# Gate columns split inside one stationary tile, new tokens' gates by one broadcast matmul, decay rows by DMA: one change to a hybrid decoder layer on Trainium2

## The chip, the cores and the metric

One NeuronCore of a Trainium2 chip. Its engines run unsynchronised, each through its own queue in order: TensorE (PE in the profile, with PEld for its weight loads), VectorE (DVE), ScalarE (ACT), GpSimd (POOL) and SyncE (SP), which here only starts DMAs. The metric is the device time of one execution in microseconds; lower is better.

## The reference

One layer of a decoder for 512 prompt tokens and 8 new tokens (520 columns), model width 1024: a half-step SwiGLU network, a token mixer, a second half-step SwiGLU network, with RMSNorm before and after each. The mixer projects its input once and runs two branches, four retention heads and four gated-delta heads of 128 channels. The change lies in the gates of the gated-delta heads:

```python
proj = (h @ w_in).astype(f32)
rq, rk, rv, rg, conv_in, gz, ga, gb, gate_r, gate_g = jnp.split(proj, idx, axis=-1)
...
beta = jax.nn.sigmoid(gb)
g_gdn = -jnp.exp(gdn_a_log.astype(f32)) * jax.nn.softplus(ga + gdn_dt_bias.astype(f32))
o_g, s_gdn_new = gated_delta_chunked(gq, gk, gv, g_gdn, beta, s_gdn.astype(f32))
```

`ga` and `gb` are four columns each, one per head. The chunked form needs `G`, the running sum of `g` within a chunk, both down the partitions (`gcol`) and as a row spread over all partitions, for the decay mask exp(G_i - G_j). New tokens need their own exp(g) and beta on all partitions.

## The kernel before, in words

Activations lie transposed: channels on partitions, the 520 tokens along the row, in two halves of 260 columns. Every product with weights is done in three passes of the fast four-byte format: weights and activations are split into a high and a low part, and high x high, high x low and low x high are summed in PSUM (`passes`, lines 404 to 410, so most matmuls have line 408, 409 or 410). A weight unit of 1024 x 128 is loaded by SyncE into one of two raw buffers, then `split` (line 340) makes the high part by a cast on ScalarE (line 350) and the low part by a subtract on VectorE (line 351). Splits are emitted by `prefetch`, up to two units ahead of the product (`AHEAD`).

The order of all work is written out by one Python program. `product` issues a unit's 48 matmuls and calls `tick` after every six. Side work is generators: each `yield n` means "go on n ticks later", and in a tick the generators' instructions are appended to their engines' queues. So a position on a queue is fixed by the tick, and an engine that falls behind meets its instructions late but in the same order. A table `LATER` (line 46) adds ticks to numbered steps of named generators, such as step 51 of the second `gdn_head`; a step is counted each time a generator yields a number above zero.

The mixer's first four units are done together by `first_units` (line 701), half by half, while the norm's factors `r` are still being made (`pre_rms`, `inverse_rms`: squares, seven adds on VectorE, line 537, sums `ss` by matmul, line 471, a power on GpSimd, and a broadcast matmul `rb`, line 477). They are: GAB, the gates' unit, in which 8 of 128 columns are used and the rest are zeros; then the key, query and value projections of gated-delta head 0 (CK, CQ, CV). When `r` is there, all four are evacuated in a row. CK, CQ and CV of heads 1 to 3 follow, then the retention units, the output gates and the branch gates. `conv` (line 1261) evacuates a unit (`cin`, line 1268) and convolves it by three VectorE operations (line 1276).

`gate_rows` (line 1164) evacuates 8 rows. `gates` (line 1170), a generator, transposes them (five transposes through line 1162), adds the bias, makes `g` and `beta` in its second step, and in its last step (from line 1214) issues one matmul with the triangle of ones (line 1215) for `gcol`, eight small matmuls that spread one head's new-token `g` or `beta` over 128 partitions (line 1218), and the copies out of PSUM (lines 1226 to 1232). The profile counts a matmul on plain four-byte data as two records, so these are 2 and 16.

`gdn_head` (line 1368) is one generator per head. Heads start their decays 48 ticks apart (`TURN`). `decays` (line 1235) spreads the head's `g` columns over the partitions while summing them, by four 128 x 128 matmuls into a PSUM bank `gbc` (line 1240), and makes from it exp(G) (`eg`), the mask `DT` (line 1247) and `ekd`. Then `inverse` (line 1484) moves blocks through DRAM by SyncE (`s1`, `L`, lines 1493 and 1499), does 31 steps of two small operations on GpSimd (lines 1513, 1514), stores by eight DMAs (line 1519), and reads back. The state is then carried over four chunks: `ks` (line 1447), `pu` (line 1453), `pS` (line 1457) and `S` (line 1459).

Of the kernel before, what the change touches and what calls it, by code (L numbers as in the profile page):

```python
# [15 lines left out]
P = 128  # L16
D = 1024
# [16 lines left out]
KH = KD // 2  # L34
PAD = CONV_W - 1
TURN = 48
WARM = 9
RAW_BUFS, SPLIT_BUFS, AHEAD = 2, 9, 2
SUM_LAG = 6
# [68 lines left out]
def units():  # L108

    out = []  # L110
    for f in (1, 2):
        for m in range(KF):
            if m < PLAIN[f]:
                out += [(f"gu{f}", 2 * m, 0, 8), (f"gu{f}", 2 * m + 1, 0, 8)]
        out += [("seven", f, m, i) for m, i in stream(PLAIN[f])]
        for d in range(KD):
            rest = [(f"dn{f}", d, 8, 15), (f"dn{f}", d, 15, 22)]
            if d in (0, KD - 1):
                out += rest + [(f"dn{f}", d, 0, 8)]
            else:  # L120
                out += rest
                if d % 2 == 0:
                    out += [("down7", f, d - 1, i) for i in range(7)]
        if f == 1:
            n = len(proj_order()) - 2 * KD
            out += [("win", i, 0, 8) for i in range(n)]
            for i in range(n, n + 2 * KD, 2):
                out += [("win", i, 0, 8), ("win", i + 1, 0, 8), ("wbr", (i - n) // 2, 0, 8)]
            out += [("wo", m, 0, 8) for m in range(KD)]
    return out  # L130

# [39 lines left out]
class Kernel:  # L171
# [95 lines left out]
    def load_to(self, j):  # L267

        nc, a = self.nc, self.a
        while self.raw_next < min(self.group[min(j, len(self.unit_list))] + RAW_BUFS, self.group[-1]):  # L270
            u = self.unit_list[self.first_of[self.raw_next]]
            if u[0] == "seven":
                w, m = a[f"gu{u[1]}"], u[2]
                s1, s3, a22 = self.begun.pop((u[1], m), None) or self.begin_pair(u[1], m)
                t = self.raw.tile([P, KD, P], F32, tag="raw", name=self.name("raw"))
                nc.sync.dma_start(out=t, in_=w[2 * m])
                t = [t[:, 0:KH], s3, None, a22, t[:, KH:KD], s1, None]
            elif u[0] == "down7":
                t = []
                for d in (u[2], u[2] + 1):  # L280
                    raw = self.raw.tile([P, KD, P], F32, tag="raw", name=self.name("raw"))
                    nc.sync.dma_start(out=raw, in_=a[f"dn{u[1]}"][d, :, 0:KD, :])
                    t += [raw[:, 0:KH], raw[:, KH:KD]]
            else:
# [119 lines left out]
    def passes(self, w, k, xhl, ps, first, last, more=False):  # L404
        hi, lo = w
        xh, xl = xhl
        mm = self.nc.tensor.matmul
        mm(ps, hi[:, k, :], xh, start=first, stop=False, skip_group_check=more)  # L408
        mm(ps, hi[:, k, :], xl, start=False, stop=False, skip_group_check=more)  # L409
        mm(ps, lo[:, k, :], xh, start=False, stop=last, skip_group_check=more)  # L410

# [752 lines left out]
    def gate_rows(self, ps):  # L1164
        rows = self.slot("rows", (P, TOK))
        for hf, (c0, n) in enumerate(HALVES):
            self.nc.vector.tensor_tensor(rows[0:8, c0 : c0 + n], ps[hf][0:8], self.r[hf][0:8], ALU.mult)
        return rows

    def gates(self, rows):  # L1170
# [2 lines left out]
        yield 4  # L1173
        pt = self.bank("gt")
        for i in range(NCH):
            self.tr(pt[:, i * 8 : i * 8 + 8], rows[0:8, i * P : (i + 1) * P])
        self.tr(pt[0:DEC, 32:40], rows[0:8, SEQ:TOK])
        ga = c.tile([P, 5, H], F32, name="ga")
        gb = c.tile([P, 5, H], F32, name="gb")
        nc.gpsimd.memset(ga, 0.0)  # L1180
        nc.gpsimd.memset(gb, 0.0)
        dt = self.vec[:, V_DT : V_DT + H]
        ptv = pt[:, 0:40].rearrange("p (c g) -> p c g", g=8)
# [29 lines left out]

        pc = self.bank("gc")
        nc.tensor.matmul(pc[:, 0:16], self.triu, g[:, 0:4, :], start=True, stop=True)
        for i, src in enumerate((g, beta)):
            for h in range(H):
                nc.tensor.matmul(
                    pc[:, 16 + (i * H + h) * DEC : 16 + (i * H + h + 1) * DEC],
                    src[0:DEC, 4, h : h + 1].to_broadcast([DEC, P]),  # L1220
                    self.ident[0:DEC, 0:DEC],
                    start=True,
                    stop=True,
                )
        self.gcol = c.tile([P, NCH, H], F32, name="gcol")
        nc.vector.tensor_copy(self.gcol, pc[:, 0:16])
        self.dgb = c.tile([P, 2, H, DEC], F32, name="dgb")
# [7 lines left out]
    def decays(self, h):  # L1235

        nc = self.nc
        pb = self.bank("gbc")
        for i in range(NCH):
            nc.tensor.matmul(  # L1240
                pb[:, i * P : (i + 1) * P], self.g[:, i, h : h + 1].to_broadcast([P, P]), self.triu, start=True, stop=True
            )
        eg = self.slot("eg", (P, NCH, P))
        nc.scalar.activation(eg, pb, AF.Exp)
        dt = self.slot("DT", (P, NCH, P))
        for i in range(NCH):
            nc.vector.scalar_tensor_tensor(
                out=dt[:, i, :],
                in0=pb[:, i * P : (i + 1) * P],
                scalar=self.gcol[:, i, h : h + 1],  # L1250
                in1=self.negm,
                op0=ALU.subtract,
# [1 line left out]
            )  # L1254
        nc.scalar.activation(dt, dt, AF.Exp)
        e = self.ekd[:, :, h]
        nc.vector.tensor_tensor(e, pb.rearrange("p (c i) -> p c i", i=P)[:, :, P - 1], self.gcol[:, :, h], ALU.subtract)
        nc.scalar.activation(e, e, AF.Exp)
        return eg, dt

# [107 lines left out]
    def gdn_head(self, h, q, k, v):  # L1368
# [408 lines left out]
def layouts(i):  # L1777
# [15 lines left out]
    blocks = []  # L1793
    for kind, h in proj_order():
        if kind == GAB:
            b = np.zeros((D, P), f)
            b[:, 0:8] = w[:, 4096:4104]
        else:
            b = w[:, start[kind] + h * P : start[kind] + (h + 1) * P]
# [78 lines left out]
```

## Time and profile before

| | |
|---|---|
| median of 3 runs | 1218.39 us (1217.87 to 1218.42) |
| span of the profiled execution | 1218.5 us |
| TensorE busy | 1189.1 us, 9937 matmul records |
| VectorE busy | 899.6 us |
| ScalarE, GpSimd busy | 573.7 us, 277.1 us |
| mean granted TensorE clock | 0.990 |
| HBM traffic | 139 GB/s over the span |

A row of a timeline gives start and duration in microseconds, the engine, the line of the kernel, the operation, and output <- input by the program's names; a matmul's shape follows, "x8" counts records, and brackets tell how long the engine stood before it and for whom. Durations of matmuls are modelled and overlap: what counts is the distance from one start to the next. A row of the waits gives who waited for whom, the total, the number and the longest. A row of the chain gives start, duration and what ran. A row of the windows gives, for a stretch, the length, each engine's busy time with its records, the granted clock, the DMA share and GB/s.

### The profile page before, as it was taken

Reading aid. Unit: us, or ns where it says so; the run is one execution under the profiler, and the core shown is the slowest. Engines: PE = TensorE matmul, PEld = TensorE weight load, DVE = VectorE, ACT = ScalarE, POOL = GpSimd, SP = SyncE. Lnnn points to the kernel's source line nnn. Section 1 sums busy time; section 2 is a strip of 40 time slices with the busy share of each in tenths; the row PEclk is TensorE's granted clock in tenths of the full one; section 3 lists DMA queues with packets and bytes.
Section 4 is the critical chain, followed back from the end, with each engine's and each line's share of the span. In section 5 each row is a group of like instructions: output and inputs, shape, how many; then the busy total and the mean of one; then the engine's idle time right before and its main releaser. Section 6 shows DMA issues by size and latency. Waiting matters only on the chain.

```text
span 1218.5 us, 25498 instructions
## 1 busy us (share of the span) xinstructions
PE 1189.1 (98%) x9937; PEld 1176.9 (97%) x9937; DVE 899.6 (74%) x1933; ACT 573.7 (47%) x1195; POOL 277.1 (23%) x502
## 2 busy tenths in 40 slices
PE   8999999999999999999999999999999999999995
PEld 7999999999999999999999999998999999999994
DVE  8988888776548787877666667546888888867554
ACT  6655666553335564313234334334565666653330
POOL 4211111000005148745541112203311111000003
PEclk8999999999999999999999999999999999999998
DMA  6787777133352533332444564342587777332352
GB/s 191 210 203 178 192 176 185 45 100 96 96 171 60 176 105 107 117 97 89 116 133 144 175 195 172 114 157 85 152 229 190 188 183 192 85 92 81 96 168 70
DMA packets 79689, 170.87 MB, mean 140 GB/s; under 512 B 17104, under 2 KB 20016, under 8 KB 79568
## 3 DMA queue, kind: packets, MB, share of 16 engines
q1 hardware_dynamic: 67280, 144.95, 37.4%
q0 software_dynamic: 12288, 24.29, 11.7%
q8 instruction: 78, 1.28, 0.4%
q14 instruction: 43, 0.35, 0.1%
HBM read 157.37 MB, written 11.83 MB: 139 GB/s over the span
## 4 chain that ended last, share of the span: by engine, by line
PE 88%; DVE 6%; ACT 2%; issue 1%; DMA 1%; POOL 1%; SPq 0%; DVEq 0%; ACTq 0%; POOLq 0%
PE sv L408 10%; PE sv L409 10%; PE sv L410 10%; PE p L408 7%; PE p L410 7%; PE p L409 7%; PE dn L408 7%; PE dn L409 7%; PE dn L410 7%; DVE wlo L351 2%; PE br L408 1%; PE br L409 1%; PE br L410 1%; PE g L409 1%; PE g L410 1%
## 5 line engine op out<-in xcount | busy, mean ns | idle before, releaser
L408 PE MATMUL p<-xhl,whi 128*128 128x260 f32 x784 | 231.0, 295 | 0.0
L409 PE MATMUL p<-xhl,whi 128*128 128x260 f32 x784 | 222.0, 283 | 1.4 <-DVE xhl L506 1.4
L410 PE MATMUL p<-xhl,wlo 128*128 128x260 f32 x784 | 221.3, 282 | 1.7 <-DVE wlo L351 1.7
L351 DVE TENSOR_TENSOR wlo<-raw,whi 128x1024 fp32r<-128x1024 f32 (+2 forms) x121 | 142.3, 1182 | 37.7 <-ACT whi L350 35.9
L408 PE MATMUL sv<-th,w 128*128 128x260 f32 x592 | 167.2, 282 | 0.5 <-ACT q L833 0.5
L409 PE MATMUL sv<-tl,w 128*128 128x260 f32 x592 | 167.1, 282 | 0.0
L410 PE MATMUL sv<-th,w 128*128 128x260 f32 x592 | 167.0, 282 | 0.0
L409 PEld LDWEIGHTS p<-xhl,whi 128*128 128x128 f32 x784 | 148.4, 189 | 2.0 <-DVE xhl L506 1.8
L410 PEld LDWEIGHTS p<-xhl,wlo 128*128 128x128 f32 x784 | 147.9, 189 | 2.1 <-DVE wlo L351 2.1
L408 PEld LDWEIGHTS p<-xhl,whi 128*128 128x128 f32 x784 | 148.1, 189 | 0.7
L350 ACT CAST whi<-raw 128x1024 fp32r<-128x1024 f32 (+2 forms) x121 | 116.4, 971 | 31.3 <-DMA raw<-dn_in 16.9
L369 DVE TENSOR_TENSOR w<-s,w 128x512 fp32r<-128x512 f32 x148 | 101.5, 688 | 37.9 <-ACT w L368 36.5
L307 POOL DMA_DIRECT2D s<-gu_in x74 | 65.1, 973 | 282.4 <-DMA s<-gu_in 143.8
L410 PE MATMUL dn<-hh,wlo 128*128 128x260 f32 x448 | 126.6, 283 | 1.2 <-DVE wlo L351 1.2
L408 PE MATMUL dn<-hh,whi 128*128 128x260 f32 x448 | 127.0, 283 | 0.0
L409 PE MATMUL dn<-hl,whi 128*128 128x260 f32 x448 | 126.7, 283 | 0.0
L409 PE MATMUL sv<-xhl,w 128*128 128x260 f32 x444 | 125.5, 283 | 0.0
L408 PE MATMUL sv<-xhl,w 128*128 128x260 f32 x444 | 125.4, 282 | 0.0
L410 PE MATMUL sv<-xhl,w 128*128 128x260 f32 x444 | 125.0, 281 | 0.0
L408 PEld LDWEIGHTS sv<-th,w 128*128 128x128 f32 x592 | 111.4, 188 | 0.9 <-ACT q L833 0.7
L410 PEld LDWEIGHTS sv<-th,w 128*128 128x128 f32 x592 | 111.6, 188 | 0.0
L409 PEld LDWEIGHTS sv<-tl,w 128*128 128x128 f32 x592 | 111.2, 188 | 0.0
(408 smaller groups left out, 3230.4 us busy)
## 6 DMA issues: line engine op xcount, KB each, us to landing
raw<-gu_in SPq DMA_DIRECT2D x50, 512.0 KB, 5.0
raw<-win_in SPq DMA_DIRECT2D x49, 512.0 KB, 3.6
s<-gu_in SPq DMA_DIRECT2D x74, 256.0 KB, 5.7
s<-gu_in POOLq DMA_DIRECT2D x74, 256.0 KB, 5.4
raw<-dn_in SPq DMA_DIRECT2D x32, 448.0 KB, 3.4
a<-gu_in SPq DMA_DIRECT2D x37, 256.0 KB, 5.9
x<-x SPq DMA_DIRECT2D x32, 260.0 KB, 5.1
raw<-dn_in SPq DMA_DIRECT2D x16, 512.0 KB, 3.7
```

Source lines behind the costliest of these rows:

```text
L307: self.nc.gpsimd.dma_start(out=out, in_=term, accum_op=ALU.add)
L350: self.nc.scalar.copy(hi[:, ks], t[:, ks])
L351: self.nc.vector.tensor_tensor(lo[:, ks], t[:, ks], hi[:, ks].bitcast(F32), ALU.subtract)
L369: nc.vector.tensor_tensor(w[:, 1], t[i], w[:, 0].bitcast(F32), ALU.subtract)
L408: mm(ps, hi[:, k, :], xh, start=first, stop=False, skip_group_check=more)
L409: mm(ps, hi[:, k, :], xl, start=False, stop=False, skip_group_check=more)
L410: mm(ps, lo[:, k, :], xh, start=False, stop=last, skip_group_check=more)
```

## The change

Four parts.

1. GAB is no longer a 128-column weight unit with a low part of its own. Its 8 columns are loaded as a small tile; high parts go into columns 0 to 7 and low parts into columns 8 to 15 of one stationary tile, the rest of which is zeroed. `passes` gets `lo` as None and issues two passes. Rows 0 to 7 and 8 to 15 of the result are added after the transposes, in `gates`. The unit list is renumbered; the unit still counts as two split buffers.
2. In the last step of `gates`, the eight small matmuls become one: VectorE multiplies `g` and `beta` of the new tokens with an identity into `diag`, and one matmul with ones spreads all 64 columns.
3. A second product with the triangle gives `G` as 16 rows of 128; VectorE copies them out (`growc`) and SyncE stores them to a DRAM tile `gscr`.
4. `decays` has no matmuls. Each head reads its four rows from `gscr`, repeated over 128 partitions (256 KB), by a SyncE DMA that is issued `ROWS_EARLY` = 12 ticks before the decays. Where there are not twelve ticks, as at head 0, which takes its turn at once, the decays come twelve ticks after the read. `LATER` is not edited.

```diff
@@ passes
+        if lo is None:
+            mm(ps, hi[:, k, :], xl, start=False, stop=last, skip_group_check=more)
+            return
@@ split
+        if self.unit_list[j][0] == "gab":
+            self.load_to(j)
+            t = self.loaded[self.group[j]]
+            both = self.whl.tile([P, KD, P], F32R, tag="w", name=self.name("both"))
+            self.started(j)
+            self.split_done[j] = (both, None)
+            self.nc.scalar.activation(both, self.ones.unsqueeze(1).to_broadcast([P, KD, P]), AF.Copy, scale=0.0)
+            self.nc.scalar.copy(both[:, :, 0:8], t)
+            self.nc.vector.tensor_tensor(both[:, :, 8:16], t, both[:, :, 0:8].bitcast(F32), ALU.subtract)
+            return
@@ gates, after the transposes (now of 16 rows)
-        nc.vector.tensor_tensor(ga[:, 0:4, :], ptv[:, 0:4, 0:4], dt.unsqueeze(1).to_broadcast([P, 4, H]), ALU.add)
-        nc.vector.tensor_tensor(ga[0:DEC, 4, :], ptv[0:DEC, 4, 0:4], dt[0:DEC], ALU.add)
-        nc.vector.tensor_copy(gb[:, 0:4, :], ptv[:, 0:4, 4:8])
-        nc.vector.tensor_copy(gb[0:DEC, 4, :], ptv[0:DEC, 4, 4:8])
+        nc.vector.tensor_copy(sb[:, 0:4, :], ptv[:, 0:4, :])
+        nc.vector.tensor_copy(sb[0:DEC, 4, :], ptv[0:DEC, 4, :])
+        nc.vector.tensor_tensor(ga, sb[:, :, 0:4], sb[:, :, 8:12], ALU.add)
+        nc.vector.tensor_tensor(gb, sb[:, :, 4:8], sb[:, :, 12:16], ALU.add)
+        nc.vector.tensor_tensor(ga, ga, dt.unsqueeze(1).to_broadcast([P, 5, H]), ALU.add)
@@ gates, last step
         nc.tensor.matmul(pc[:, 0:16], self.triu, g[:, 0:4, :], start=True, stop=True)
+        nc.tensor.matmul(pc[0:16, P : 2 * P], g[:, 0:4, :], self.triu, start=True, stop=True)
+        diag = self.small("dg", [P, 2, H, DEC])
+        eye = self.ident[0:DEC, 0:DEC].unsqueeze(1).to_broadcast([DEC, H, DEC])
         for i, src in enumerate((g, beta)):
-            for h in range(H):
-                nc.tensor.matmul(
-                    pc[:, 16 + (i * H + h) * DEC : 16 + (i * H + h + 1) * DEC],
-                    src[0:DEC, 4, h : h + 1].to_broadcast([DEC, P]),
-                    self.ident[0:DEC, 0:DEC],
-                    start=True,
-                    stop=True,
-                )
+            nc.vector.tensor_tensor(diag[0:DEC, i], src[0:DEC, 4, :].unsqueeze(2).to_broadcast([DEC, H, DEC]), eye, ALU.mult)
+        nc.tensor.matmul(pc[:, 16:80], self.ones[0:DEC, :], diag[0:DEC], start=True, stop=True)
+        grow = self.slot("growc", (16, P))
+        nc.vector.tensor_copy(grow, pc[0:16, P : 2 * P])
+        self.gscr = self.dram.tile([NCH, H, P], F32, name="gscr")
+        nc.sync.dma_start(out=self.gscr.rearrange("c h i -> (c h) i"), in_=grow)
@@ decays: its four matmuls become a read
+    def decay_rows(self, h):
+
+        t = self.slot("gbc", (P, NCH, P))
+        self.nc.sync.dma_start(out=t, in_=self.gscr[:, h, :].unsqueeze(0).to_broadcast([P, NCH, P]))
+        return t
@@ gdn_head
-        if turn > self.now:
-            yield turn - self.now
-        eg, DT = self.decays(h)
+        if turn - ROWS_EARLY > self.now:
+            yield turn - ROWS_EARLY - self.now
+        rows = self.decay_rows(h)
+        yield max(turn, self.now + ROWS_EARLY) - self.now
+        eg, DT = self.decays(h, rows)
```

More of the change, by code (lines that the diff above doesn't have):

```diff
@@ L36 @@
 TURN = 48
+ROWS_EARLY = 12
 WARM = 9
@@ L125, in units @@
             n = len(proj_order()) - 2 * KD
-            out += [("win", i, 0, 8) for i in range(n)]
+            out += [("gab", 0, 0, 8)] + [("win", i, 0, 8) for i in range(n - 1)]
             for i in range(n, n + 2 * KD, 2):
-                out += [("win", i, 0, 8), ("win", i + 1, 0, 8), ("wbr", (i - n) // 2, 0, 8)]
+                out += [("win", i - 1, 0, 8), ("win", i, 0, 8), ("wbr", (i - n) // 2, 0, 8)]
             out += [("wo", m, 0, 8) for m in range(KD)]
@@ L283, in load_to @@
                     t += [raw[:, 0:KH], raw[:, KH:KD]]
+            elif u[0] == "gab":
+                t = self.slot("gabw", (P, KD, 8))
+                nc.sync.dma_start(out=t, in_=a["gab"])
             else:
@@ L1166, in gate_rows @@
         for hf, (c0, n) in enumerate(HALVES):
-            self.nc.vector.tensor_tensor(rows[0:8, c0 : c0 + n], ps[hf][0:8], self.r[hf][0:8], ALU.mult)
+            self.nc.vector.tensor_tensor(rows[0:16, c0 : c0 + n], ps[hf][0:16], self.r[hf][0:16], ALU.mult)
         return rows
@@ L1233, in gates, with decays @@
         self.ekd = c.tile([P, NCH, H], F32, name="ekd")
-    def decays(self, h):
-        nc = self.nc
[L1238 to L1242, printed above, removed]
+    def decay_rows(self, h):
+        t = self.slot("gbc", (P, NCH, P))
+        self.nc.sync.dma_start(out=t, in_=self.gscr[:, h, :].unsqueeze(0).to_broadcast([P, NCH, P]))
+        return t
+    def decays(self, h, pb):
+        nc = self.nc
         eg = self.slot("eg", (P, NCH, P))
@@ L1248, in decays @@
                 out=dt[:, i, :],
-                in0=pb[:, i * P : (i + 1) * P],
+                in0=pb[:, i, :],
                 scalar=self.gcol[:, i, h : h + 1],
@@ L1256, in decays @@
         e = self.ekd[:, :, h]
-        nc.vector.tensor_tensor(e, pb.rearrange("p (c i) -> p c i", i=P)[:, :, P - 1], self.gcol[:, :, h], ALU.subtract)
+        nc.vector.tensor_tensor(e, pb[:, :, P - 1], self.gcol[:, :, h], ALU.subtract)
         nc.scalar.activation(e, e, AF.Exp)
@@ L1795, in layouts @@
         if kind == GAB:
[L1796 to L1799, printed above, removed]
+            out["gab"] = asc(w[:, 4096:4104].reshape(KD, P, 8).transpose(1, 0, 2))
+            continue
+        b = w[:, start[kind] + h * P : start[kind] + (h + 1) * P]
         blocks.append(b.reshape(KD, P, P).transpose(1, 0, 2))
```

10 lines of the change are left out of this document (5 added, 5 removed).

## The prediction

> **What bounds the kernel now.** I read the page first, then what TensorE waits for.
>
> ```profile
> span 1218.5 us, 25498 instructions
> PE 1189.1 (98%) x9937; PEld 1176.9 (97%) x9937; DVE 899.6 (74%) x1933; ACT 573.7 (47%) x1195; POOL 277.1 (23%) x502
> PE p L410 <- DVE wlo L351: 1.7, 2, 1.4
> ```
>
> TensorE is busy for 98% of the span, so matmuls taken out should shorten it, unless TensorE comes to wait for another engine where they stood. Its waits are few today; the 1.4 us one for `wlo` lies in the stage that the change edits. So I read the chain of waits there, then VectorE and TensorE in order of time.
>
> ```profile
> 399.21 0.66 DVE rows L1167 x2
> ...
> 411.18 1.23 DVE wlo L351
> 412.45 0.39 PE p L410
> ...
> 420.71 1.88 PE gc L1218 x16
> ```
>
> From 399 to 412 us VectorE carries the chain: the four leading units get their factors `r` all at once, and it works off their evacuations and convolutions. TensorE runs ahead and is caught once, at 412.45. How far behind VectorE stays is seen where the gates' last stage stands (first fence TensorE, second VectorE):
>
> ```profile
> 420.42 0.29 PE L1215 MATMUL gc<-gg,cst 128*128 128x16 f32 x2
> ...
> 422.51 2.08 PE L1240 MATMUL gbc<-cst,gg 128*128 128x128 f32 x8
> 424.25 0.57 PE L408 MATMUL p<-xhl,whi 128*128 128x260 f32 x1
> 424.61 0.42 PE L409 MATMUL p<-xhl,whi 128*128 128x260 f32 x1
> 424.82 0.42 PE L410 MATMUL p<-xhl,wlo 128*128 128x260 f32 x1
> ```
>
> ```profile
> 425.57 0.42 DVE L1268 TENSOR_TENSOR cin<-p,rb 128x260 f32<-128x260 f32 x1
> 427.11 2.75 DVE L1276 SCALAR_TENSOR_TENSOR cv<-cin,vec,cv 128x512 f32<-128x512 f32 x3 [0.72 <-ACT cv L1274]
> 429.77 1.23 DVE L351 TENSOR_TENSOR wlo<-raw,whi 128x1024 fp32r<-128x1024 f32 x1
> 430.93 0.16 DVE L1226 COPY gcol<-gc 128x16 f32<-128x16 f32 x1
> 431.35 0.19 DVE L1229 COPY dgb<-gc 128x32 f32<-128x32 f32 x1 [0.26 <-ACT dgb L1228]
> ```
>
> TensorE issues the gates' matmuls at 420.42. The first thing that VectorE is given in the same step, the `gcol` copy, runs at 430.93 with no wait before it: VectorE is 10 us behind, on an evacuation, a convolution and a weight split that were emitted earlier. Today that costs nothing, because no matmul of this step reads anything VectorE makes in it. It is this that the change alters.
>
> **Part by part.** *GAB unit.* Its third pass goes: 8 k x 2 halves = 16 matmuls.
>
> ```profile
> 379.00 0.39 PE L410 MATMUL p<-xhl,wlo 128*128 128x260 f32 x1 [0.33 <-DVE wlo L351]
> 391.56 1.51 DVE L537 TENSOR_TENSOR sq<-sq,sq 128x520 f32<-128x520 f32 x2
> 393.45 0.28 PE L410 MATMUL p<-xhl,wlo 128*128 128x260 f32 x1
> 393.57 1.02 PE L471 MATMUL ss<-ones,sq 128*87 128x1 f32 x12
> ```
>
> Matmuls of this form start 0.12 us apart (393.45 to 393.57), so on paper 1.92 us go. The first half's 0.96 us are worth nothing: they lie ahead of 379.00, where TensorE stands for another unit's split whenever it arrives. The second half's 0.96 us bring the sums `ss` to 392.61, but the last `sq` add ends at 393.07; with hand-over I take 393.12. From `ss` the chain runs through `r` to 412.45 without TensorE's products, so 0.45 us is what everything after gains. The new split (a zero fill and a narrow copy on ScalarE, a narrow subtract on VectorE) replaces a full cast and subtract long before the unit is due; the load shrinks; neither was waited for by TensorE. I cost them at zero; were that cover gone, about one such subtract, 1.23, would be exposed.
>
> *Gate rows, transposes, gates.* The transposes stay five; wider ones cost nothing, by L1215, whose 16 columns take 0.11 a record where L1218's 8 take 0.12. VectorE gets five small operations for four ahead of the last stage: +0.15 us, by the 0.16 of `gcol`. ScalarE, 47% busy, may load its exponential table twice more, since head 0's exponentials move away from this step's; no matmul waits for that.
>
> *The last stage.* Out go the 16 records of L1218 and head 0's 8 of L1240 (422.51). In come a second product of `g` with `triu` (2 records, 0.22 by L1215) and one broadcast matmul of `diag`. The two multiplies that make `diag` are emitted in the same step, so they stand on VectorE's queue exactly where `gcol` stands now, behind the 429.77 split. TensorE arrives at 420.42 - 0.45 + 4 records x 0.11 = 420.41. VectorE arrives at 430.93 - 0.45 + 0.15 = 430.63 and needs about 0.3 for two operations like `dgb`'s 0.19: 430.9. TensorE stands for 10.5 us. Behind the waiting matmul is the rest of this unit's product, that is, all of TensorE's work; who would wait for that, VectorE and ScalarE, are draining their own backlog, so nothing on them gets faster for it. With 0.3 for the matmul the product resumes at 431.2, where it resumed at 424.25: +6.95.
>
> *Clock.* The windows view (granted clock third from the right):
>
> ```profile
> 15.00:19.70 4.70, 4.70 (x23) 4.70 (x23) 4.70 (x11) 3.82 (x11) 1.64 (x3) 0.50 0.43 122
> 19.80:24.00 4.20, 4.20 (x37) 4.20 (x37) 3.78 (x8) 2.08 (x5) 0.00 (x0) 1.00 0.42 120
> 422.60:425.90 3.30, 3.30 (x15) 3.30 (x16) 3.24 (x6) 2.93 (x18) 1.64 (x2) 0.50 0.76 286
> 426.00:440.00 14.00, 14.00 (x121) 14.00 (x121) 11.36 (x32) 10.40 (x29) 5.96 (x8) 1.00 0.27 76
> 13.77 0.59 PE L409 MATMUL g<-xhl,whi 128*128 128x260 f32 x1 [0.62 <-DVE xhl L506]
> ```
>
> After the stretch of tiny matmuls the granted clock fell to 0.50 for 3.3 us; the products from 424.25 to 425.9 ran 0.21 apart (424.61 to 424.82) instead of 0.12: eight of them, 0.75 us lost. That loss goes. But a stand of 10 us must bring the clock down too. What recovery costs is bounded by the two stretches here: 3.3 us at half speed, 1.65 lost; or, from the last start-up wait (13.77) to 19.7, 5.9 us, 3.0 lost. I take the middle, 2.3. Net +1.55. The Trainium skill (TensorE: Matmul & The Clock Gate, Part 1) says the gate opens after one busy window of about 3.4 us; by that alone the loss would be some 1.7, an estimate, and the sum 0.6 lower; the start-up rows show a longer stretch, so the middle stands.
>
> *Heads 1 to 3.* Their broadcasts on TensorE go.
>
> ```profile
> 463.05 1.05 PE L1240 MATMUL gbc<-cst,gg 128*128 128x128 f32 x8
> 463.86 0.37 PE L408 MATMUL p<-xhl,whi 128*128 128x260 f32 x1
> 464.06 0.28 PE L409 MATMUL p<-xhl,whi 128*128 128x260 f32 x1
> 569.11 1.06 PE L1240 MATMUL gbc<-cst,gg 128*128 128x128 f32 x8
> ```
>
> Each takes 0.81 (463.05 to 463.86) and a re-entry 0.08 over pitch (0.20 for 0.12): 0.89, and no wait stands nearby to swallow it. Three: -2.7. The Trainium skill (same page, Back-to-back issue gap) gives about 81 ns per matmul of 128 columns in a stream; by that, an estimate, the 24 records are worth 1.9 and the sum is 0.8 higher. The rows show 0.81 per eight, so they decide.
>
> In their place each head reads 256 KB of rows by SyncE twelve ticks ahead; the nearest rows are the inverse's own broadcast loads:
>
> ```profile
> L1499 SPq DMA_DIRECT2D L<-s x8: 520/551/601, 446.5 to 583.7; - x8
> DMA to landing us min/median/max: 3.1/3.5/4.3
> SPq L1519 <- POOL TT L1524: 11.2, 4, 6.2
> ```
>
> 4.3 us at most against twelve ticks. Turns are 48 ticks apart and head 0's stood at 422.51, head 1's at 463.05, so a tick is 0.85 and twelve are 10 us: hidden, if SyncE is free. For head 0 the write of `growc` and the read follow VectorE's 431; any load emitted later is emitted by a product that stood still as well. Zero; its ends are none and the 4 us of the second rival.
>
> *Moved steps.* Head 0 starts twelve ticks later, and each head has one more counted step, so the hand-set corrections of LATER fall one step early. For head 1 the 7 - 3 shortened wait moves to the wait between writing `S` and the matmul that reads it, which falls from 5 ticks to 1.
>
> ```profile
> 599.40 0.39 PE L1467 MATMUL go<-AT,qk 128*128 128x128 f32 x2
> 600.57 0.33 DVE L1459 SCALAR_TENSOR_TENSOR S<-S,egl,pS 128x128 f32<-128x128 f32 x1
> 606.03 0.38 PE L1447 MATMUL ks<-S,cv 128*128 128x128 f32 x2
> ```
>
> One tick of six products (0.72) after 599.62 is 600.35; `S` is done at 600.90: a wait of 0.5. The other corrections move inside loops with slack. Between nothing and 2; I take 0.5.
>
> *Sum.* +6.95 +1.55 -2.7 +0.5 = +6.3 on the profiled 1218.5, which is 0.1 above the median of the three runs. So 1224.7.
>
> **Rivals.** *The matmul finds `diag` ready.* If VectorE reached the last stage with TensorE, the step would cost 0.25 after 420.41, resuming at 420.66 against 424.25 (-3.6), with the 0.75 of clock gone and -2.7 from the heads and 0.5 back: 1211.9. For it speaks that TensorE is 98% busy and loses some 50 records; against it the 430.93 row. It decides by VectorE's lag: gain and loss cross at a wait of about 4.3 us, taking 2.3 for the clock; the rows have 10.5. If the two multiplies slipped in ahead of 425.57, the wait would be near 5, and the time 1219, no change.
>
> *Rows late.* SyncE issues in order. Head 0's inverse, twelve ticks later, puts its eight stores in front of head 2's rows, and such stores waited for GpSimd up to 6.2 us. With that and the 3.5 of landing, head 2's rows would come about 4 us after their turn; ScalarE's exponentials and VectorE stop, and TensorE loses up to those 4 us at the next split it needs: 1228.7. For it speaks the 6.2, against it that splits are made two units ahead, which is why I cost it at zero.
>
> **How the numbers follow.** My forecast 0.74; `diag` ready 0.09; half the wait, no change, 0.07; rows late 0.10. A measurement of this kernel can tell about 0.2% (2.4 us) from no change. Faster 0.09, same 0.08, slower 0.83. The forecast's own range: low with 1.65 for the clock, no extra step and VectorE 1 us sooner, 1222.5; high with 3.0 and 2 us of moved steps, 1226.9. Taking in the late rows, and on the low side a shorter lag: 1221.5 to 1229.5.
>
> **What would show it.** Right: TensorE waits some 10 us for the `diag` tile in one piece near 420 us, the clock at 0.50 for 3 to 6 us after it, the `ss` sums only 0.5 us sooner, `gcol` again near 431, head turns without matmuls. Wrong: no wait at that matmul, or TensorE's stand made up by fewer waits before 600 us, or new waits for the row transfers.

## The result and the profile after

| | before | after |
|---|---|---|
| median, on the same chip | 1218.41 us (1217.87 to 1219.99) | 1235.14 us (1234.54 to 1235.8) |
| ratio, 95% interval | | 1.0139 (1.0126 to 1.0151) |
| profiled execution, span | 1218.5 us | 1234.0 us (time 1235.8) |
| mean granted TensorE clock | 0.990 | 0.985 |

The change makes the kernel slower by 16.7 us. The forecast was slower by 6.3, 1221.5 to 1229.5 at its ends: the sign is right, the size far off. The clock means leave out the first 6.1 us of the kernel before and the first 16.7 us of the kernel after, for which the traces hold no clock record (the windows view prints 1.00); matmuls stand 0.21 us apart there, as they do at half clock. One execution of a kernel in experiment 8, of 2964.56 us, is left out of its ratio.

The page's head for the kernel after (busy time, share of the span, instructions):

```profile
span 1234.0 us, 25386 instructions
PE 1190.7 (96%) x9877; PEld 1177.2 (95%) x9877; DVE 903.6 (73%) x1937; ACT 577.0 (47%) x1198; POOL 275.0 (22%) x501
```

TensorE issues 60 records fewer and its busy time still doesn't fall (1189.1 before). Records that run at half clock last longer (0.42 us instead of 0.28 for a product's matmul in the rows below), so busy time hides a clock loss. The view of waits for TensorE, kernel after:

```profile
PE gc L1239 <- DVE dg L1238: 10.5, 1, 10.5
PE cb L1636 <- POOL gdm L1633: 3.7, 1, 3.7
PE g L426 <- DVE xhl L523: 2.8, 5, 1.0
```

The first line is the stand that was forecast. The second is new and was not: the matmul `cb` of the new tokens' norm waits 3.7 us for a power, `gdm`, on GpSimd. The rest are much as before. TensorE's order of time around both, kernel after:

```profile
418.75 0.37 PE L1233 MATMUL gc<-gg,cst 128*128 128x16 f32 x2
419.06 0.39 PE L1234 MATMUL gc<-cst,gg 128*16 128x128 f32 x2
429.90 0.69 PE L1239 MATMUL gc<-dg,ones 8*128 8x64 f32 x2 [10.45 <-DVE dg L1238]
430.52 0.59 PE L422 MATMUL p<-xhl,whi 128*128 128x260 f32 x1
...
505.93 0.28 PE L427 MATMUL p<-xhl,wlo 128*128 128x260 f32 x1
509.92 0.69 PE L1636 MATMUL cb<-cst,gdm 64*128 64x64 f32 x2 [3.71 <-POOL gdm L1633]
510.53 0.58 PE L422 MATMUL p<-xhl,whi 128*128 128x260 f32 x1
510.91 0.42 PE L426 MATMUL p<-xhl,whi 128*128 128x260 f32 x1
511.13 0.42 PE L427 MATMUL p<-xhl,wlo 128*128 128x260 f32 x1
```

And VectorE at the first of them, kernel after:

```profile
428.41 1.24 DVE L365 TENSOR_TENSOR wlo<-raw,whi 128x1024 fp32r<-128x1024 f32 x1
429.57 0.17 DVE L1238 TENSOR_TENSOR dg<-gg,cst 8x32 f32<-8x32 f32 x1
429.67 0.17 DVE L1238 TENSOR_TENSOR dg<-beta,cst 8x32 f32<-8x32 f32 x1
430.62 0.28 DVE L1241 COPY growc<-gc 16x128 f32<-16x128 f32 x1 [0.78 <-PE gc L1239]
430.83 0.15 DVE L1245 COPY gcol<-gc 128x16 f32<-128x16 f32 x1
```

The two multiplies run directly behind the weight split, where `gcol` stood before. The windows view of after (length, then busy time and records of PE, PEld, DVE, ACT, POOL, then granted clock, DMA share, GB/s) shows, between start-up and the end, three stretches at half clock where before had one of 3.4 us:

```profile
422.90:436.50 13.60, 6.60 (x29) 6.48 (x30) 7.32 (x22) 6.47 (x15) 5.56 (x6) 0.50 0.35 112
436.60:508.20 71.60, 69.61 (x584) 69.25 (x583) 57.98 (x142) 35.72 (x89) 39.49 (x96) 1.00 0.34 98
508.30:515.10 6.80, 5.18 (x23) 5.07 (x24) 2.06 (x10) 0.00 (x0) 5.77 (x19) 0.50 0.35 65
515.20:614.00 98.80, 98.31 (x888) 96.43 (x886) 70.32 (x214) 28.14 (x55) 47.55 (x126) 1.00 0.33 104
614.10:617.40 3.30, 3.30 (x17) 3.23 (x17) 2.28 (x6) 0.88 (x3) 0.00 (x0) 0.50 0.55 144
```

To see where the time comes, I subtract the start of a product's matmul before from the start of the same matmul after (both streams hold the same product matmuls, `p` in the mixer and `sv` in the networks, counted from the last one):

| TensorE's place (time in before) | after minus before, us | step |
|---|---|---|
| first network (52.5 to 236.5) | -1.2 | start-up, put down to the clock (last section) |
| ahead of the gates' last stage (405.2) | -1.65 | GAB -0.45 |
| 25 us past it (449.5) | +8.4 | the stand for `diag` and its clock, +10.05 |
| past head 1's turn (476.9) | +7.6 | its decay matmuls gone, -0.8 |
| ahead of `cb` (496.3) | +7.7 | |
| ahead of head 3's turn (564.9) | +12.25 | +4.55: head 2 -0.8, eight records of the heads' state (`pu`, `pS`, `go`) that come later in this stream -0.9, so `cb`'s stand and its clock +6.25 |
| past it (587.9) | +11.4 | -0.8 |
| past the third stretch at half clock (606.5) | +14.0 | +2.6, of which 1.7 clock and 0.9 those eight records |
| end of the projections (786.0) | +14.4 | |
| end of the second network's gates (1073.4) | +15.4 | +1.0, matmul pitch, the distance from one start to the next (last section) |
| span | +15.5 | |

Without the start-up row it is +16.7, which is what the medians say.

### The profile page after: what moved, and what is told of

It is laid out like the page before. It is cut to its first block, busy times and chain, and to the rows that moved or that the text cites. A ratio compares the mean times of both kernels' runs of the same rounds, so it can differ in the third digit from the quotient of the medians.

```text
span 1234.0 us, 25386 instructions
## 1 busy us (share of the span) xinstructions
PE 1190.7 (96%) x9877; PEld 1177.2 (95%) x9877; DVE 903.6 (73%) x1937; ACT 577.0 (47%) x1198; POOL 275.0 (22%) x501
## 4 chain that ended last, share of the span: by engine, by line
PE 77%; DVE 11%; ACT 5%; issue 2%; POOL 2%; DMA 1%; SPq 0%; DVEq 0%; ACTq 0%; POOLq 0%
PE sv L422 10%; PE sv L426 10%; PE sv L427 10%; PE dn L422 6%; PE dn L427 6%; PE dn L426 6%; PE p L422 5%; PE p L426 5%; PE p L427 5%; DVE wlo L365 2%; PE br L422 1%; ACT whi L364 1%; PE br L426 1%; PE br L427 1%; DVE cv L1296 1%
## 5 line engine op out<-in xcount | busy, mean ns | idle before, releaser
L422 PE MATMUL p<-xhl,whi 128*128 128x260 f32 x768 | 228.6, 298 | 0.0
L426 PE MATMUL p<-xhl,whi 128*128 128x260 f32 x768 | 219.7, 286 | 0.0
```

## The experiments

The main theory, **A**: each stand comes from a place on a queue. `diag` stands behind VectorE's backlog; `gdm` stands late on GpSimd's queue because head 0's inverse now starts twelve ticks later. The rivals: **B**, the `gdm` stand is an echo of the `diag` stand, so it goes with it; **C**, the row transfers come late and hold ScalarE and VectorE; **D**, VectorE and ScalarE bound 400 to 465 us anyway, so what TensorE gains there it gives back at the next wait; **E**, the later stands come from `LATER` being off by one step; **F**, the gates' thinner unit makes the clock fall; **G**, a removed stand reappears at the next GpSimd or VectorE result (experiment 5's expectation uses the letter G for another theory). All runs of `before` beside them had medians of 1217.87 to 1218.78.

**1. `diag` multiplied earlier.** In the kernel after, the multiplies move ahead of the generator's wait of 13 ticks, to where `g` and `beta` are made:

```diff
         self.beta, self.g = beta, g
+        diag = c.tile([P, 2, H, DEC], F32, name="dg")
+        (the two multiplies)
         yield 13
```

Expected: 

> The changed kernel with one difference: the two multiplies that make diag are issued right after beta, one generator step (13 ticks) earlier. Theory A (the stand of 10.5 us comes from the place of diag on VectorE's queue; the second stand, for GpSimd's gdm, comes from head 0 starting twelve ticks later): the 10.5 us wait and the clock loss of about 3 us behind it go, the wait for gdm of 3.7 us and its clock loss stay. 1235.1 - 10.5 - 3.0 = about 1221.5. Theory B (everything else that was lost after 430 us follows from that one stand, which displaces the engines against each other): the wait for gdm goes too, about 1214 to 1216.

Measured: 1229.93 us, ratio 1.0096 (1.0081 to 1.0111). TensorE finds `diag` ready, yet wins 5.2 us, not 10.5. The view of waits, and a stretch of TensorE's timeline, of this kernel:

```profile
PE cb L1636 <- POOL gdm L1633: 5.9, 1, 5.9
```

```profile
433.05 0.39 PE L422 MATMUL p<-xhl,whi 128*128 128x260 f32 x1 [0.26 <-DVE dgb L1248]
441.82 0.39 PE L422 MATMUL p<-xhl,whi 128*128 128x260 f32 x1 [0.96 <-ACT s L1401]
448.39 0.39 PE L427 MATMUL p<-xhl,wlo 128*128 128x260 f32 x1 [0.66 <-DVE wlo L365]
```

TensorE was 5.5 us ahead of the kernel before at 438 us and level with it at 462. Of this, 1.6 is head 0's sixteen `pa` records, which come later here and so were only put off; 3.2 are four pauses in the product, from 432.5, 440.6, 447.5 and 455.0 us, of which the rows show three. TensorE has caught up with ScalarE and VectorE. Then it stands 5.9 us for `gdm` instead of 3.7. So the first stand had hidden part of what comes behind it; both numbers expected were wrong (1221.5 by A, 1214 to 1216 by B).

**2. Each part by itself**, three kernels made from the kernel before. `only_diag` has part 2 alone, `only_gab` part 1 alone, `only_rows` parts 3 and 4 alone with the sixteen records of small matmuls kept:

```diff
only_diag
-        (the eight small matmuls)
+        (the two multiplies)
+        nc.tensor.matmul(pc[:, 16:80], self.ones[0:DEC, :], diag[0:DEC], start=True, stop=True)
only_rows
+        nc.tensor.matmul(pc[0:16, P : 2 * P], g[:, 0:4, :], self.triu, start=True, stop=True)
+        (growc, gscr, decay_rows, decays on its rows, gdn_head's two waits)
```

Expected, `only_diag`: 

> The kernel before with part 2 alone: diag by VectorE and one broadcast matmul in place of the sixteen records; gate unit and decays as before. Theory A: one stand of about 10.5 us near 421, clock at half for some microseconds behind it, head 0's four decay matmuls behind that, no wait for gdm: 1218.4 + 6.3 to 6.9 at the resume, + 2.3 clock, + 0.9 for the decay matmuls = 1227 to 1229. Theory B: the wait for gdm appears here as well, 1232 to 1236.

Expected, `only_gab`: 

> The kernel before with part 1 alone: eight gate columns' high and low parts in one stationary tile, sixteen matmuls fewer; last step of the gates and decays as before. Both theories: only what lies between the last wait for a split at 379 us and the sums at 393 us is gained, 0.45 us: 1218.0, no wait for gdm. If all sixteen matmuls counted, 1216.5.

Expected, `only_rows`: 

> The kernel before with parts 3 and 4 alone: G as rows through DRAM, decay rows by DMA twelve ticks ahead, head 0 twelve ticks later; the sixteen records for the new tokens and the gate unit as before. Theory A: no 10 us stand, but the wait for gdm (3.7 us) with its clock loss (2.5) and the later half-clock stretch (1.7) appear; gained are 2.0 at head 0 and 2.7 at the others: 1218.4 - 4.7 + 0.2 + 7.9 = about 1222. Theory B: no stand, so no wait for gdm: about 1214. Theory C (the row transfers themselves come late and hold ScalarE and VectorE): waits of ScalarE for the rows of several microseconds, and TensorE waits for splits.

| | us | ratio, 95% interval | long waits of TensorE | half clock between start-up and end, us |
|---|---|---|---|---|
| `only_diag` | 1229.37 | 1.0089 (1.0072 to 1.0106) | `diag` 10.5 | 422.8 to 436.4 |
| `only_gab` | 1222.01 | 1.0030 (1.0018 to 1.0042) | none new | 371.8 to 378.6, 423.0 to 426.4 |
| `only_rows` | 1229.56 | 1.0093 (1.0078 to 1.0108) | `gdm` 5.9 | 423.1 to 426.5, 501.6 to 508.4, 607.4 to 610.8 |

Each part by itself is slower than before. `only_diag` lies 0.4 above A's range, with A's single stand and no wait for `gdm`. `only_rows` has the `gdm` stand without any `diag` stand before it, so B falls; ScalarE waits for none of its row transfers, which landed in 3.5 to 5.1 us, so C falls too. That the rows cost 11 us on their own missed A as well: the stand is 5.9 where A took 3.7, and the 6.8 and 3.4 us at half clock behind it lose 5.1. What the missing decay records gain is spent before that: TensorE is 1.2 us ahead of the kernel before at 420 us and 0.7 at 496, with new waits of 0.5 (`cin`) and 0.8 (`gsq`).

`only_gab` missed too, and its trace explains the loss only in part. The windows view of it and of `gab_third_pass` (experiment 5) for the same stretch:

```profile
371.80:378.60 6.80, 6.80 (x36) 6.80 (x35) 5.61 (x10) 5.86 (x14) 3.05 (x5) 0.50 0.08 29
```

```profile
371.80:378.60 6.80, 6.32 (x50) 5.91 (x51) 5.83 (x11) 5.49 (x12) 3.37 (x5) 1.00 0.09 17
```

The leading units' stage is paced by the activations there (TensorE waits 1.16 us for `xhl` at 371.4). Two units are done together, and with one of their six passes taken out the clock was at half for 6.8 us. That cost 1.0 us: a lead of 1.3 us on the kernel before at 365 us should have grown by 0.35, as it did in the kernel after, and was 0.7 at 405. Another 2.0 us go between 430 and 1073 us, where nothing was edited, mostly as a longer pitch, and just as many in `gab_third_pass`.

**3. Head 0 with its matmuls.** In the kernel after, head 0 makes its rows by the four old matmuls and starts its decays at once; heads 1 to 3 read theirs. The second kernel has `diag` early too.

```diff
-        if turn - ROWS_EARLY > self.now:
+        if h == 0:
+            rows = self.decay_products(h)
+        else:
             (the two waits and the read)
```

Expected, `head0_products`: 

> The changed kernel, but head 0 takes its decay rows by four matmuls at once, as the kernel before does, and so does not start twelve ticks later; heads 1 to 3 read theirs by DMA. Theory A (the wait for gdm comes from head 0's twelve ticks, which put its GpSimd steps in front of decode_gdn's power): the stand for diag stays at 10.5 us, no matmul waits for gdm, the clock loss behind it goes: 1235.1 - 3.9 - 2.6 + 0.9 = 1229.5 or, with the half-clock stretch near 614 gone too, 1228. Theory B (the stand for diag displaces the engines): the wait for gdm stays, 1236.

Expected, `early_head0_products`: 

> As head0_products, and diag is multiplied one step earlier, so neither stand should be there. If the two stands were all that the change lost: the kernel before less 2.7 (heads 1 to 3), less 2.3 (small matmuls and their clock loss), plus 2 to 3.6 that the gate unit alone cost: 1216 to 1218. Theory D (VectorE, some 10 us behind from 400 to 460 us, bounds this stage, and TensorE cannot use time that is freed on it): TensorE waits for weight splits between 425 and 460 us and gives most of it back, 1218 to 1221.

Measured: 1230.29 us, 1.0101 (1.0084 to 1.0118), and 1224.16 us, 1.0050 (1.0031 to 1.0070). The view of one tile, `gdm`, tells why (VectorE makes the input, GpSimd takes the power; the start is next to last). Before, after, and `head0_products`:

```profile
L1609 DVE TENSOR_SCALAR gdm<-cs x1: 140/140/140, 495.5 to 495.5; 64x1 f32<-64x1 f32 x1
L1611 POOL TENSOR_TENSOR gdm<-gdm,mhalf x1: 568/568/568, 497.3 to 497.3; 64x1 f32<-64x1 f32 x1
```

```profile
L1631 DVE TENSOR_SCALAR gdm<-cs x1: 136/136/136, 503.6 to 503.6; 64x1 f32<-64x1 f32 x1
L1633 POOL TENSOR_TENSOR gdm<-gdm,mhalf x1: 570/570/570, 509.3 to 509.3; 64x1 f32<-64x1 f32 x1
```

```profile
L1643 DVE TENSOR_SCALAR gdm<-cs x1: 140/140/140, 501.1 to 501.1; 64x1 f32<-64x1 f32 x1
L1645 POOL TENSOR_TENSOR gdm<-gdm,mhalf x1: 569/569/569, 503.0 to 503.0; 64x1 f32<-64x1 f32 x1
```

From input to power it takes 1.8 us before, 5.7 after, and 1.9 with head 0 in its old place. In `only_rows` and `diag_early`, where head 0 is late, it is 5.6 each; in `early_head0_products` 1.8. What fills the queue is seen on GpSimd's timeline. First the end of head 0's 62 small operations in the kernel before, then the kernel after from the same operation on:

```profile
486.29 0.21 POOL L1514 TENSOR_TENSOR pack<-pack 128x4 f32<-128x4 f32 x1
```

```profile
503.23 0.21 POOL L1536 TENSOR_TENSOR pack<-pack 128x4 f32<-128x4 f32 x1
503.38 0.24 POOL L1535 TENSOR_TENSOR pack<-L,pack 128x30 f32<-128x30 f32 x1
...
506.63 0.53 POOL L1546 MEMSET TT<- 128x512 f32 x1
507.09 0.31 POOL L1549 MEMSET pack<- 64x256 f32 x1
507.37 1.03 POOL L1535 TENSOR_TENSOR pack<-L,pack 128x25 f32<-128x25 f32 x1
...
509.10 0.24 POOL L1536 TENSOR_TENSOR pack<-pack 128x24 f32<-128x24 f32 x1
509.29 0.57 POOL L1633 TENSOR_TENSOR gdm<-gdm,mhalf 64x1 f32<-64x1 f32 x1
```

GpSimd has no pause in this stretch. Before, head 0's inverse began on GpSimd at 449.75 and its small operations ended at 486.5; after, 462.78 and 503.4, when the input of `gdm` is about to come (503.6). The `pack` rows from 503.38 on are head 1's. Seven such pairs stand ahead of the power on the queue in both kernels, but before four of them had run when its input came (495.5); after, none was done, and the two MEMSETs that end head 0's inverse are still to run too. `head0_products` loses 0.5 us on the kernel before between 496 and 640 us where the kernel after loses 6.3, both with one later stretch at half clock: 5.8 is the price of the stand and its clock in these two traces. In `early_head0_products` the stands are down to 1.7 us (for `dgb`) and 2.1 (for `gdm`), and it is still slower than before and above both ranges expected.

**4. LATER renumbered.** In the kernel after, the entries of heads 0 to 2 are moved up by one step (one of three lines shown):

```diff
-    ("gdn_head", 1): {0: 3, 51: 1, 52: -3},
+    ("gdn_head", 1): {0: 3, 52: 1, 53: -3},
```

Expected: 

> The changed kernel with the corrections of LATER for gdn_head 0 to 2 moved one step on, so that they fall on the steps that they were made for. Theory A: the waits for diag and gdm stay as they are; at most 0.5 to 2 us near 570 to 620 are won: 1233 to 1235. Theory E (the misplaced corrections cause the loss after 500 us): the wait for gdm goes, 1228.

Measured: 1233.33 us, 1.0126 (1.0111 to 1.0141): 1.8 us under the kernel after, both stands unchanged (10.4 and 3.7). E falls as the cause of the stands and the time is inside A's range. The numbering is worth 1.8 us at most: this trace has 3.4 us at half clock behind `cb` instead of 6.8 and no stretch near 614 us, 3.4 us less lost, enough for all of it.

**5. The gates' unit with a third pass.** `only_gab` with a pass on a tile of zeros, so that it has as many matmuls as before:

```diff
-            self.split_done[j] = (both, None)
+            zero = self.whl.tile([P, KD, P], F32R, tag="w", name=self.name("zero"))
+            self.nc.gpsimd.memset(zero.bitcast(F32), 0.0)
+            self.split_done[j] = (both, zero)
```

Expected: 

> Part 1 alone (1222.0 as measured), but the gate unit's sixteen matmuls of the third pass are issued after all, on a stationary tile of zeros, so that TensorE has as many matmuls as before and all else of part 1 stays. Theory F (in the stage where TensorE is paced by the activations, two thirds of the matmuls for one of two units let the granted clock fall to half): the half-clock stretch of 6.8 us near 372 us is gone, 1219 to 1220. Theory G (part 1's loss lies in the new splits, rows or slots): 1222 to 1224.

Measured: 1220.11 us (1218.68 to 1223.38), 1.0021 (1.0011 to 1.0030), against 1.0030 (1.0018 to 1.0042) for `only_gab`. The profile has the full clock at 372 us, as the second row in experiment 2 shows. That fits F, but the intervals overlap: suggested, not shown. The other traces leave F half standing. None of the seven kernels with all three passes has a fall of the clock there. Of the seven with the thinner unit three have one (`only_gab`; `head0_products` and `later_renumbered` for 3.4 us), and in the last two TensorE gains 0.35 us on the kernel before from 365 to 405 us like the four without one, so there it cost nothing. This trace also has the full clock at 423 us, where the clock of `only_gab` fell behind the same matmuls.

**6. The stand at `cb` alone.** In the kernel after, only the wait between the power and `cb` is longer; GpSimd's queue is untouched.

```diff
-    ("decode_gdn", 0): {1: 8, 2: 2, 10: 3},
+    ("decode_gdn", 0): {1: 8, 2: 2, 3: 6, 10: 3},
```

Expected: 

> The kernel after, with one entry added to LATER: the wait between the new-token power (gdm, on GpSimd) and the matmul cb that reads it is 11 ticks instead of 5. Nothing on GpSimd's queue moves. Theory A (the 3.7 us stand at cb is the second cost of the change, caused by the power's late place behind head 0's inverse, and it brings a drop of the granted clock worth 2.6): the stand goes, the half-clock stretch near 508 us goes, 1235.1 - 3.7 - 2.6 = 1228.8, 1228 to 1230. Theory G (the stand only hides another lag, of VectorE behind TensorE, which comes up at the next matmul that reads a VectorE result): the stand moves, and the time stays within 2 us of the kernel after, 1233 to 1235.

Measured: 1229.01 us, 1.0087 (1.0074 to 1.0100): 6.1 us less than the kernel after, the number of A. How it comes about is less clean. TensorE's timeline of this kernel has a smaller stand in its place:

```profile
511.12 0.55 PE L1368 MATMUL po<-st,rp 128*128 128x128 f32 x2 [1.85 <-POOL rp L1347]
```

`rp` is the operation right behind `gdm` on GpSimd. So 1.85 of the 3.71 moves on, as G said, the clock falls for 3.4 us (511.4 to 514.8) instead of 6.8, and the stretch near 614 us doesn't occur. Against the kernel after, TensorE is 3.0 us ahead at 565 us (by the place in before), 4.3 at 640, past the missing stretch, and 5.7 at 1073, with a shorter pitch in the second network; the span is 5.1 us shorter. So only 3.0 of it comes from the stand and its clock, and that the total meets A's number is partly luck.

**7. The broadcast at its best.** The kernel before with the eight small matmuls replaced by one whose operand is a constant, so that it never waits; the new tokens' `g` and `beta` are thereby not spread.

```diff
-        (the eight small matmuls)
+        nc.tensor.matmul(pc[:, 16:80], self.ones[0:DEC, :], self.ident[0:DEC, 0:64], start=True, stop=True)
```

Expected: 

> The kernel before, with the eight small matmuls (16 records) replaced by one broadcast matmul of 64 columns whose operand is a constant (a piece of the identity), so that it never waits. The new tokens' g and beta are thereby not spread: that part of the computation is left out. It is part 2 of the change at its very best. Theory A alone (TensorE's own time is what counts): 14 records and the half-clock stretch at 422 us go, 1.6 + 0.75 = 2.4 us, 1215.5 to 1216.5. Theory D (VectorE and ScalarE lag by some 10 us there, so TensorE gives back what it gains, at a conv's or a split's result it needs before 465 us): within 1 us of the kernel before, 1217.5 to 1219.

Measured: 1220.17 us (1217.39 to 1222.62), 1.0009 (1.0000 to 1.0017): no gain. The number lies above both ranges, nearer to D's. The trace bears out D's reason for a part: TensorE was 0.2 us ahead of the kernel before at 420 us and 3.3 at 430, gave back 1.15 of this by 449, and was still 2.0 ahead at 588. At 606 it was 0.45 ahead. The one new line of the waits, at 431.4 us, and the windows view of this kernel:

```profile
PE tr L1162 <- DVE dgb L1221: 0.5, 1, 0.5
```

```profile
596.50:599.80 3.30, 3.30 (x30) 3.14 (x29) 2.65 (x8) 0.37 (x2) 1.73 (x4) 1.00 0.09 13
599.90:603.30 3.40, 3.40 (x18) 3.34 (x18) 1.79 (x5) 1.53 (x3) 2.64 (x10) 0.50 0.15 24
```

The half-clock stretch at 422 us went, and one came up at 600 us, behind sixteen one-column matmuls (`sp`), and cost 1.6. In before, the same sixteen ran without a drop. That the one replaced the other is not shown: `heads123_rows` and `gab_third_pass` keep the small matmuls at 422 us and have neither stretch.

**8. Heads 1 to 3 alone.** The kernel before with rows read for heads 1 to 3, the read in a generator of its own so that no step is renumbered; the second kernel has the early `diag` as well.

```diff
+        rows = []
+        if h:
+            self.spawn(self.read_rows(h, rows, turn))
         if turn > self.now:
             yield turn - self.now
-        eg, DT = self.decays(h)
+        rows = rows[0] if h else self.decay_products(h)
+        eg, DT = self.decays(h, rows)
```

Expected, `heads123_rows`: 

> The kernel before, with the rows read by DMA for heads 1 to 3 alone: head 0 keeps its four matmuls and its place, the eight small matmuls stay, and the reads are emitted by generators of their own, so every numbered step keeps its number and LATER fits as before. Added: the second triangle product (2 records), one copy, one store, three reads. Theory A (each head's matmuls cost 0.89 us of TensorE's time, and nothing else of part 4 costs if head 0 isn't delayed): -2.7 + 0.25 = 1216.0, 1215 to 1217, no stand at cb, no new wait. Theory D (what TensorE gains is given back at waits for VectorE): waits of some 2 us come up behind heads 1 to 3 and the time stays at 1218 to 1219.

Expected, `heads123_early`: 

> The kernel heads123_rows with the eight small matmuls replaced by the broadcast matmul of diag, whose two VectorE multiplies stand one generator step (13 ticks) earlier: parts 2, 3 and 4 without the two stands, and the old GAB unit. Theory A: the terms add, 1218.4 - 2.7 + 0.25 - 1.6 - 0.75 = 1213.6, 1213 to 1215. Theory D: the gain of the broadcast matmul is given back before 465 us, 1216 to 1218, and the waits between 425 and 465 us show it.

Measured: 1220.02 us, 1.0012 (1.0003 to 1.0020), and 1225.51 us (1218.35 to 1229.12), 1.0047 (1.0032 to 1.0062). Both lie above both ranges expected. The view of waits of `heads123_rows` has four new lines, and that of `heads123_early` two of more than 1 us:

```profile
PE cb L1640 <- POOL gdm L1637: 0.7, 1, 0.7
PE pX L1591 <- DVE pack L1587: 0.5, 1, 0.5
...
PE po L1370 <- POOL pack L1539: 0.2, 1, 0.2
PE tr L1163 <- DVE dgb L1235: 0.2, 1, 0.2
```

```profile
PE cb L1636 <- POOL gdm L1633: 1.9, 1, 1.9
...
PE tr L1163 <- DVE dgb L1231: 1.7, 1, 1.7
```

In the first, the four waits take 1.6 of the 2.7 us that the heads' matmuls were worth, much as D said. TensorE ends its projections 2.0 us ahead of the kernel before, of which it had 0.7 at 420 us, ahead of the edit, and loses 1.1 in the second network by a longer pitch. In the second, TensorE comes 2 us sooner and meets VectorE and GpSimd, which don't; three half-clock stretches follow (499.3 to 506.1, 571.0 to 574.4, 605.1 to 608.5). No version made here has a median below that of the kernel before.

## Why the prediction was wrong

**GAB unit.** Forecast -0.45; the table has -0.45, of which 0.35 between 365 and 405 us. That alone this part measures +3.6 (`only_gab`) was not foreseen; its trace accounts for 1.0 by the clock at 372 us and 2.0 after 430 us. The kernel after's own profile has the full clock at 372 us, so in that execution the part did not cost the 1.0.

**The last stage.** TensorE arrived at 418.75, the wait was 10.45 (forecast 10.5), and the reason was the one given: `diag` ran where `gcol` had stood. From the first matmul of the stage to the product's return took 11.77 (418.75 to 430.52) against 3.83 before (420.42 to 424.25): +7.94, or +7.5 with GAB's gain, where the forecast was +6.95 with it. The 0.55 more lies in two places: the broadcast took 0.62 to the product's next start, at half clock, where I put 0.3, and the two triangle products took 0.70 (418.75 to the wait's begin, 429.90 - 10.45) where I put 0.44. Term right, a little small.

**Clock.** Forecast +1.55 net. From the same table, 10.05 - 7.94 = +2.1. The product came back at 430.52 and the clock at 436.5: 6.0 us at half, 3.0 lost, the upper bound that the start-up rows gave, less the old 0.75. Even the old loss is not in every execution: `heads123_rows` keeps the small matmuls and ran on at the full clock.

**Heads 1 to 3.** Forecast -0.89 each; the table has -0.8 and -0.8. Right on TensorE's own time. The reason given for counting it in full, that no wait stands nearby to swallow it, was wrong: in experiment 8 four new waits swallow 1.6, and the median gains nothing.

**Row DMAs.** Forecast zero. They landed in 3.4 to 4.4 us and no engine waited for them.

**Moved steps: the step that failed.** I put them at +0.5, "between nothing and 2", and looked at what the numbered corrections do and at SyncE's queue. The same sentence says that head 0 starts twelve ticks later; I didn't follow the 62 small operations of its inverse onto GpSimd's queue and ask what they then hold up. They hold up head 1's operations and with them the power for the new tokens, whose matmul had about 0.5 us to spare before (power done 497.9, `cb` at 498.4). That gave a stand of 3.7 and 2.6 of clock behind it (5.2 us at half after 509.92); +6.25 in the table, where +0.5 was forecast. Experiment 3 shows the cause, since with head 0 back in its place the stand is gone, and a price of 5.8; experiment 6 confirms the price only in part. The rival that came nearest, rows late, started from the right backlog (GpSimd's, up to 6.2, made later by head 0's inverse), but looked for its price on SyncE's queue, where no one waited.

**What no step held.** A third fall of the clock (+1.7 near 614 us) and a longer pitch in the second network (+1.0). The rivals "ready" and "half the wait", and the forecast for the heads, took for granted that time freed on TensorE is time won. Experiments 7 and 8 say otherwise: no kernel with fewer records came out ahead of the kernel before. Where the time went was read from one profile each (waits for VectorE and GpSimd, clock, pitch); it is not shown for every execution of kernels whose runs scatter by 3 to 11 us.

**The base.** The prediction sets the profiled span, 1218.5, beside the median of 1218.39. A run's time is about 1.8 us longer than its span (1235.8 for 1234.0 after), so the profiled execution of before was one of the longer ones; the late end of its start-up (last section) fits this. The sum of 1224.7 is not touched by it.

Side by side: forecast +6.95 + 1.55 - 2.7 + 0.5 = +6.3; measured, by the table, +7.5 + 2.1 - 2.4 + 6.25 + 1.7 + 1.4 = +16.55. Of the difference of 10.25, 5.75 is in the moved steps, 3.1 in the fall of the clock near 614 us and what comes after it, which no term held, and 1.4 in the two sizes and the heads. With the moved steps right the sum would have been about 1230.4, an estimate by the table, still short of 1235.

## What to carry to other kernels

When a step starts later, list its operations on every engine, and for each engine name the next operation behind them on its queue that some other engine needs: in this case the price was there, not at the step. A TensorE that is 98% busy is not thereby the only bound; ask at the next three or four places where it needs another engine how much that engine has in hand, because a gain upstream can be spent there. Before replacing tiny matmuls by one that needs a fresh operand, look where that operand's producer stands on its queue when the consumer arrives.

## What the runs showed of the hardware

The clock's stretches at half speed, other than the one that each trace ends in, came in whole multiples of one length: 3.41, 6.83, 10.24 and 13.65 us in these traces. The Trainium skill (TensorE: Matmul & The Clock Gate, Part 1) describes free-running windows of 3413 ns; the traces agree. The 1.2 us at start-up fit this: both streams begin at 1.02 us, and the last start-up stretch at half speed ends at 19.75 in before and at 16.75 in after. The same part of the Trainium skill lets the clock fall after an idle window. Here less was enough: in `power_later` it fell at 511.43 after a single wait of 1.85 us, in `only_gab` at 371.8 with TensorE busy for 2.21 of the 3.40 us ahead. It also fell while the records have TensorE busy throughout: before at 422.5 behind 26 short records (3.40 of 3.40), `ready_spread` at 599.9 (3.30 of 3.30). And it did not fall each time: `gab_third_pass` has the same 26 short records near 422 us as before, `heads123_rows` two more, and both the full clock. What the gate counts as busy is not shown.

The pitch of the same 1510 matmuls in the second network lay between 119.9 and 120.8 ns in the fourteen programs (120.1 before, 120.8 after, 119.9 in `power_later`), though nothing in them was edited. That is up to 1.4 us between programs; the cause is open, and it is as large as several terms that were argued over here.
